# Norm 2's factor spread in two steps, and two unread products behind the attention: a decoder block on one core

## The chip, the cores and the metric

The kernel runs on one core of one Trainium2 chip. A core has a matrix engine (PE in the rows; its weight loads have their own rows, PEld), a vector engine (DVE), a scalar engine (ACT), GpSimd (POOL) and a queue that issues most transfers (SP). The metric is the time of one execution on the device in microseconds (us), the median of several runs.

## What is computed

One layer of a decoder block on 256 tokens of width 2048, in float32. The part around the change, cut from the reference:

```python
h = rms_norm(x, norm1_w[l])
proj = h @ w_in[l]
...                                   # attention (o_nsa) and gated DeltaNet (o_dn) from proj
g_nsa, g_dn = jnp.split(jax.nn.sigmoid(merge_g), 2, axis=-1)
mixed = g_nsa * (o_nsa @ w_up_nsa[l]) + g_dn * (o_dn @ w_up_dn[l])
x = x + mixed @ w_o[l]
h2 = rms_norm(x, norm2_w[l])
x = x + (jax.nn.silu(h2 @ w_ffn_gate[l]) * (h2 @ w_ffn_up[l])) @ w_ffn_down[l]
return rms_norm(x, norm_f_w)
```

`rms_norm` divides each token's row by the root of its mean square. The hidden width of the last three products (the feed-forward part) is 5632.

## The kernel before, in words

**Products.** Weights are read from memory once, in chunks of 1 MB (`load`). Each float32 operand is split into a rounded part `hi` and a remainder `lo` (`split`: ACT writes `hi`, DVE writes `lo`), both of a 4-byte type that TensorE takes in one record per product. A product of two such operands is made of three: hi times hi, lo times hi and hi times lo. An ordinary float32 product, without the split, shows in the trace as two records. A transpose through the identity shows as one.

**Two shapes of the main loop.** `group_t` multiplies with the weights as stationary operand: its line L234 issues products with 256 moving columns. A chunk has two halves; each half issues 24 such products, 16 on `hi` and 8 on `lo`, and then calls `pump`. `group` has the activations as stationary operand and 512 moving columns, on L260, L261 and L262. In the order of the program, the stretches that matter here are:

- the products of the first big matrix on the normalised input (tile `hh`), 256 wide for the most part, with the small products of DeltaNet and attention between them;
- `wud` and `wun` (tiles `odn`, `onsa`): 16 calls of `group_t`, 768 products of 256 columns;
- `wo` (tile `xa`): four calls of `group`, 4 x 4 x 4 x 2 x 3 = 384 products of 512 columns, with transposes of the sum `x1t` on L1196;
- gate and up of the feed-forward part (`wfg`, tile `h`): 88 chunks, 4224 products of 256 columns;
- down (`wd`, tiles `fa` and `fxy`): 4 x 11 x 4 x 2 x 3 = 1056 products of 512 columns.

**What is put between.** Side work runs as Python generators: `pump`, called after each half chunk, takes one step of each lane. So a `yield` moves work by half a chunk. `keep_in_program_order` (`pin`) keeps an instruction at its place on its engine. The attention (`nsa_q`) is such a generator; its last product is `cmp_values` on L923 (tile `oacc`, 96 rows, 512 columns, of the split type).

**Norm 2's factor.** The sum of squares is known when `wo` ends. DVE computes the inverse root in a chain of small operations (`rsqrt`, L275 to L279, tile `r_y`). `row_bcast` then spreads the factors of the two halves of the tokens over the partitions: for each half one float32 product of the broadcast factor with the identity (L1053, tile `R`), and one copy out of PSUM by DVE (L1055). Here the generator that calls it:

```python
def bcast2():
    for _ in range(3):
        yield
    self.R2b = row_bcast(r2, "R2")[:, None, :].to_broadcast([P, 2, 256])
```

It is taken up behind the fourth half chunk of gate and up, where the first gate tile is complete; that tile is multiplied with `R2b` on L1231.

Of the kernel before, what the change touches and what calls it, by code (L numbers as in the profile page):

```python
# [14 lines left out]
P = 128  # L15
# [80 lines left out]
class Kern:  # L96
# [284 lines left out]
    def conv_in(self, e, half, pre):  # L381

        V = self.nc.vector
        if half == 0:
            pre = self.ar.alloc([4, 260], "zm")
            V.memset(pre[:, :, 0:3], 0.0)
        V.tensor_tensor(pre[:, 2 * half:2 * half + 2, 3:259], e, self.R[:, None, :].to_broadcast([P, 2, 256]), op=OP.mult)
        return pre
# [333 lines left out]
    def nsa_kv(self):  # L722
# [16 lines left out]
        kc, vc, ks, kw = self.kvT  # L739
        V.tensor_tensor(vc.ap, vc.ap, self.R[:, None, :].to_broadcast([P, 2, 256]), op=OP.mult)  # L740
        for x in (kc, ks, kw):
# [71 lines left out]
    def nsa_q(self):  # L813
# [141 lines left out]
                yield  # L955
        for v in self.vn:
            v.free()


    def build(self):  # L960
# [82 lines left out]
        def norm_factor(ss, name):  # L1043
            v = self.small([2], name + "v")
            V.tensor_scalar(v[:], ss, 1.0 / D, EPS, op0=OP.mult, op1=OP.add)
            r = self.rsqrt(v[:], [2], name)
            return r

        def row_bcast(r, name):

            bank = self.aux(name)
            for tt in range(2):
                self.pin(nc.tensor.matmul(bank[:, tt * P:(tt + 1) * P], r[:, tt:tt + 1].to_broadcast([P, P]), self.cs["ident"], start=True, stop=True))  # L1053
            R = self.cp.tile([P, 256], F32, name=name)
            V.tensor_copy(R[:], bank[:, :256])  # L1055
            return R

# [4 lines left out]
        rstd1 = self.small([2], "rstd1")  # L1062

        def evac_zab(g, ps):
            w = ZAB_W[g]
            o = 40 if g == 0 else 0
            z0 = sum(ZAB_W[:g]) + o - 40
            for tt in range(2):
                if g == 0:
                    V.tensor_scalar(ab[:, tt, :], ps[tt][:, 0:16], rstd1[:, tt:tt + 1], None, op0=OP.mult)  # L1070
                    V.tensor_scalar(self.gat[:, tt, :], ps[tt][:, 16:40], rstd1[:, tt:tt + 1], None, op0=OP.mult)
                nc.scalar.activation(self.zs[:, tt, z0:z0 + w - o], ps[tt][:, o:w], AF.Silu, scale=rstd1[:, tt:tt + 1])
# [19 lines left out]
        def rms1(ps):  # L1092
            ss = self.small([2], "ssx1")
            V.tensor_reduce(ss[:], ssx[:], axis=AX.X, op=OP.add)
            v = norm_factor(ss[:], "r1")
            V.tensor_copy(rstd1[:], v[:])
            xT.free()
            xn.free()
            evac_zab(0, ps[0])
            yield  # L1100
            evac_zab(1, ps[1])
            yield
            self.R = row_bcast(rstd1, "R1")
            yield from self.dn_small(ab)

        zab = [[t[f"zab{g}"][c] for c in range(4)] for g in range(3)]
        self.add(rows_in())
        ps = self.pair(zab[:2], hact, ZAB_W, first)
        self.add(rms1(ps))
        ps = self.group(zab[2], hact, ZAB_W[2])  # L1110
        evac_zab(2, ps)
# [16 lines left out]
        for n in ("rc", "rs"):  # L1128
            V.tensor_tensor(self.cs[n], self.cs[n], self.R[:], op=OP.mult)

# [55 lines left out]
        for g in range(4):  # L1186
            ps = self.group([t["wo"][g * 4 + c] for c in range(4)], mact)
            cs = slice(g * 512, g * 512 + 512)
            for tt in range(2):
# [3 lines left out]
                bank = self.aux("x1T")  # L1193
# [8 lines left out]
        r2 = norm_factor(sst[:], "r2")  # L1202

        def bcast2():
            for _ in range(3):
                yield
            self.R2b = row_bcast(r2, "R2")[:, None, :].to_broadcast([P, 2, 256])

        self.add(bcast2())
        h2 = lambda k: hh[k // 4][:, :, k % 4, :]  # L1210

# [173 lines left out]
```

## Time and profile before

| | before |
|---|---|
| time, median of 3 runs | 1486.42 us (1485.66 to 1487.04) |
| time of the profiled execution | 1486.53 us |
| its span, first to last instruction | 1484.7 us |
| PE busy, share of the span | 99% |
| DVE, ACT, POOL busy | 61%, 46%, 5% |
| mean granted TensorE clock | 0.998 of full speed |
| DMA, mean rate | 188 GB/s |

The time exceeds the span by 1.8 us, which lies outside the instructions. PE's busy share says little by itself: its records are pipelined, each lasts longer than the distance to the next one, and so a PE that is busy all the time can still issue its products at one distance or another. That distance is read from the start times of rows.

### The profile page before, as it was taken

Reading aid. Unit: us, or ns where it says so; the run is one execution under the profiler, and the core shown is the slowest. Engines: PE = TensorE matmul, PEld = TensorE weight load, DVE = VectorE, ACT = ScalarE, POOL = GpSimd, SP = SyncE. Lnnn points to the kernel's source line nnn. Section 1 sums busy time; section 2 is a strip of 40 time slices with the busy share of each in tenths; the row PEclk is TensorE's granted clock in tenths of the full one; section 3 lists DMA queues with packets and bytes.
Section 4 is the critical chain, followed back from the end, with each engine's and each line's share of the span. In section 5 each row is a group of like instructions: output and inputs, shape, how many; then the busy total and the mean of one; then the engine's idle time right before and its main releaser. Section 6 shows DMA issues by size and latency. Waiting matters only on the chain.

```text
span 1484.7 us, 25996 instructions
## 1 busy us (share of the span) xinstructions
PE 1470.0 (99%) x11017; PEld 1404.8 (95%) x11017; DVE 901.9 (61%) x1352; ACT 688.7 (46%) x850; POOL 78.7 (5%) x69
## 2 busy tenths in 40 slices
PE   9999999999999999999999999999999999999997
PEld 8999999999999999998899999999999998888886
DVE  5679996676787755556655555455555454445444
ACT  5655444445455546444444444444444444444343
POOL 1000101000000000210000000000000000000000
PEclk9999999999999999999999999999999999999999
DMA  8754546345554455455555555555555556555553
GB/s 333 243 195 171 185 171 199 119 166 207 191 194 148 143 199 198 171 199 173 196 178 192 187 182 195 177 196 176 194 185 185 193 179 225 188 188 194 196 198 114
DMA packets 41541, 279.20 MB, mean 188 GB/s; under 512 B 5056, under 2 KB 5584, under 8 KB 9552
## 3 DMA queue, kind: packets, MB, share of 16 engines
q1 hardware_dynamic: 38880, 270.08, 51.9%
q10 hardware_dynamic: 1440, 4.82, 0.9%
q0 software_dynamic: 1104, 2.64, 0.8%
q8 instruction: 86, 1.41, 0.4%
q14 instruction: 31, 0.25, 0.1%
HBM read 274.62 MB, written 2.89 MB: 187 GB/s over the span
## 4 chain that ended last, share of the span: by engine, by line
PE 94%; DVE 3%; DMA 1%; ACT 0%; issue 0%; SPq 0%; DVEq 0%; ACTq 0%
PE mm L234 63%; PE mm L261 8%; PE mm L262 8%; PE mm L260 8%; DVE lo L160 1%; DMA raw<-in_zab 1%; PE oacc L917 1%; PE U L587 1%; DVE main L398 1%; PE pt L903 0%; DVE xs L489 0%; DVE xs L491 0%; PE x1T L1196 0%; PE hid L770 0%; PE hid L771 0%
## 5 line engine op out<-in xcount | busy, mean ns | idle before, releaser
L160 DVE TENSOR_TENSOR lo<-raw,hi 128x1024 fp32r<-128x1024 f32 (+2 forms) x510 | 617.7, 1212 | 440.3 <-ACT hi L159 439.5
L159 ACT ACTIVATE hi<-raw 128x1024 fp32r<-128x1024 f32 (+2 forms) x510 | 533.8, 1048 | 673.1 <-PE mm L234 411.3
L234 PE MATMUL mm<-h,hi 128*128 128x256 f32 x2816 | 360.7, 281 | 0.0
L234 PEld LDWEIGHTS mm<-h,hi 128*128 128x128 f32 x2816 | 344.0, 189 | 0.1
L234 PE MATMUL mm<-hh,hi 128*128 128x256 f32 x2304 | 291.5, 279 | 0.0
L234 PEld LDWEIGHTS mm<-hh,hi 128*128 128x128 f32 x2304 | 275.1, 188 | 0.6 <-ACT hi L159 0.2
L234 PE MATMUL mm<-h,lo 128*128 128x256 f32 x1408 | 194.5, 281 | 0.0
L234 PEld LDWEIGHTS mm<-h,lo 128*128 128x128 f32 x1408 | 178.3, 189 | 0.0
L234 PE MATMUL mm<-hh,lo 128*128 128x256 f32 x1152 | 155.3, 277 | 0.0
L234 PEld LDWEIGHTS mm<-hh,lo 128*128 128x128 f32 x1152 | 142.3, 188 | 0.0
L262 PE MATMUL mm<-hi,fxy 128*128 128x512 f32 x192 | 74.7, 389 | 0.0
L261 PE MATMUL mm<-lo,fxy 128*128 128x512 f32 x192 | 74.7, 389 | 0.0
L260 PE MATMUL mm<-hi,fxy 128*128 128x512 f32 x192 | 74.7, 389 | 0.0
L1233 POOL TENSOR_TENSOR sgt<-sgt,R 128x512 f32<-128x512 f32 x22 | 33.6, 1527 | 548.8 <-ACT sgt L1232 548.8
L260 PE MATMUL mm<-hi,fa 128*128 128x512 f32 x160 | 62.3, 389 | 0.0
L262 PE MATMUL mm<-hi,fa 128*128 128x512 f32 x160 | 62.2, 389 | 0.0
L261 PE MATMUL mm<-lo,fa 128*128 128x512 f32 x160 | 62.2, 389 | 0.0
L261 PE MATMUL mm<-lo,xa 128*128 128x512 f32 x128 | 50.1, 391 | 0.0
L262 PE MATMUL mm<-hi,xa 128*128 128x512 f32 x128 | 50.1, 391 | 0.0
L260 PE MATMUL mm<-hi,xa 128*128 128x512 f32 x128 | 49.8, 389 | 0.0
L261 PE MATMUL mm<-lo,hh 128*128 128x354 f32 (+2 forms) x128 | 44.7, 350 | 0.6 <-DVE lo L160 0.5
L260 PE MATMUL mm<-hi,hh 128*128 128x354 f32 (+2 forms) x128 | 44.1, 351 | 1.2 <-ACT hi L146 1.2
(341 smaller groups left out, 1358.5 us busy)
## 6 DMA issues: line engine op xcount, KB each, us to landing
raw<-in_wfg SPq DMA_DIRECT2D x88, 1024.0 KB, 4.7
raw<-in_wd SPq DMA_DIRECT2D x44, 1024.0 KB, 4.7
raw<-in_wmg SPq DMA_DIRECT2D x32, 1024.0 KB, 4.7
raw<-in_wdn SPq DMA_DIRECT2D x24, 1024.0 KB, 4.8
raw<-in_nsa SPq DMA_DIRECT2D x16, 1024.0 KB, 4.8
raw<-in_wo SPq DMA_DIRECT2D x16, 1024.0 KB, 4.8
raw<-in_wud SPq DMA_DIRECT2D x8, 1024.0 KB, 4.8
raw<-in_wun SPq DMA_DIRECT2D x8, 1024.0 KB, 4.8
```

The costliest lines, as they stand in the source:

```text
L159: nc.scalar.activation(hv, rv[:, m * h:m * h + m, :], AF.Copy)
L160: nc.vector.tensor_tensor(lv, rv[:, m * h:m * h + m, :], hv.bitcast(F32), op=OP.subtract)
L234: nc.tensor.matmul(ps[:, f], (hv, hv, lv)[p][:, k, f * P:f * P + P], a[:, p % 2, :], start=c + h + p + k == 0, stop=c == n - 1 and h + p + ...
L260: nc.tensor.matmul(o, a[:, 0, sl], hv[:, k, :], start=begin, stop=False)
L261: nc.tensor.matmul(o, a[:, 0, sl], lv[:, k, :], start=False, stop=False)
L262: nc.tensor.matmul(o, a[:, 1, sl], hv[:, k, :], start=False, stop=last)
L398: V.scalar_tensor_tensor(cT[:, f, :], pre[:, f, j:j + 256], cw[:, o + j:o + j + 1], cT[:, f, :], op0=OP.mult, op1=OP.add)
L587: nc.tensor.matmul(bv[:, j, :], Pm[t, hg][:, j, :], U[t, hg][:, j, :], start=True, stop=True)
L917: nc.tensor.matmul(ov[:, j, :], self.vn[kb][:, c:c + 128], pt[:, br * nb + kb, :], start=j == 0 and br == 0 and kb == 0, stop=False, skip_ ...
L1233: nc.gpsimd.tensor_tensor(sgt[:], sgt[:], self.R2b, op=OP.mult)
```

## The change

`row_bcast` becomes a generator. With `steps=2`, used for norm 2 alone, it yields between its two products, so that one half chunk of gate and up stands between them; `bcast2` waits two steps in place of three, so the second product stays where the pair stood and the first moves half a chunk forward. A new `kick` issues two float32 products of the identity with itself into a PSUM bank that nothing reads, behind the attention's last product.

```diff
         for v in self.vn:
             v.free()
+        self.kick()
+
+    def kick(self):
+
+        bank = self.aux("kick")
+        for _ in range(2):
+            self.pin(self.nc.tensor.matmul(bank[:, :P], self.cs["ident"], self.cs["ident"], start=True, stop=True))
...
-        def row_bcast(r, name):
+        def row_bcast(r, name, steps=1):
 
             bank = self.aux(name)
             for tt in range(2):
                 self.pin(nc.tensor.matmul(bank[:, tt * P:(tt + 1) * P], r[:, tt:tt + 1].to_broadcast([P, P]), self.cs["ident"], start=True, stop=True))
+                if tt == 0 and steps == 2:
+                    yield
...
-            self.R = row_bcast(rstd1, "R1")
+            self.R = yield from row_bcast(rstd1, "R1")
...
         def bcast2():
-            for _ in range(3):
+            for _ in range(2):
                 yield
-            self.R2b = row_bcast(r2, "R2")[:, None, :].to_broadcast([P, 2, 256])
+            R2 = yield from row_bcast(r2, "R2", 2)
+            self.R2b = R2[:, None, :].to_broadcast([P, 2, 256])
```

On PE, at the end of the attention, these instructions stood before the change (`mm` are the main loop's PSUM tiles; what stands in brackets is whom an instruction waits for):

```order
L234 MATMUL mm_6370<-hh,lo_6470 128x256 [waits DVE_49]
L234 MATMUL mm_6370<-hh,lo_6470 128x256 x7
L923 MATMUL oacc_6232<-zkh 128x512 [waits DVE_49]
L234 MATMUL mm_6503<-odn,hi_6506 128x256 [waits Activation_49]
L234 MATMUL mm_6503<-odn,hi_6506 128x256 x15
```

and these now:

```order
L234 MATMUL mm_6370<-hh,lo_6470 128x256 [waits DVE_49]
L234 MATMUL mm_6370<-hh,lo_6470 128x256 x7
L923 MATMUL oacc_6232<-zkh 128x512 [waits DVE_49]
L964 MATMUL kick_6501<-consts 128x128 x2
L234 MATMUL mm_6506<-odn,hi_6509 128x256 [waits Activation_49]
L234 MATMUL mm_6506<-odn,hi_6509 128x256 x15
```

The two products stand directly behind L923, with no main-loop product between and with no wait of their own.

On PE, at the start of gate and up (third and fourth half chunk, then the first of the next tile), these stood before:

```order
L234 MATMUL mm_8172<-h_7509,lo_8234 128x256 x7
L234 MATMUL mm_8172<-h_7509,hi_8261 128x256 [waits Activation_49]
L234 MATMUL mm_8172<-h_7509,hi_8261 128x256 x7
L234 MATMUL mm_8172<-h_7509,hi_8261 128x256 [waits DVE_49]
L234 MATMUL mm_8172<-h_7509,hi_8261 128x256 x7
L234 MATMUL mm_8172<-h_7509,lo_8262 128x256 x8
L1053 MATMUL R_8289<-consts,r_y_8159 128x128 [waits DVE_49,PE_49]
L1053 MATMUL R_8289<-consts,r_y_8159 128x128
L234 MATMUL mm_8298<-h_7509,hi_8301 128x256 [waits Activation_49]
```

and these now:

```order
L234 MATMUL mm_8175<-h_7512,lo_8237 128x256 x7
L1060 MATMUL R_8264<-consts,r_y_8162 128x128 [waits DVE_49,PE_49]
L234 MATMUL mm_8175<-h_7512,hi_8266 128x256 [waits Activation_49]
L234 MATMUL mm_8175<-h_7512,hi_8266 128x256 x15
L234 MATMUL mm_8175<-h_7512,lo_8267 128x256 x8
L1060 MATMUL R_8264<-consts,r_y_8162 128x128
L234 MATMUL mm_8301<-h_7512,hi_8304 128x256 [waits Activation_49]
```

The first product of the pair, with its wait for DVE's chain, now stands 24 products earlier; the second stands where it stood. On DVE, ACT, POOL and SP every instruction keeps its place.

## Rows read from the trace of the kernel before

**Rows 1.** The profile's page: the span, the busy time of PE and its weight loads, and the granted TensorE clock in 40 slices (9 is 90% or more).

```profile
span 1484.7 us, 25996 instructions
PE 1470.0 (99%) x11017; PEld 1404.8 (95%) x11017; DVE 901.9 (61%) x1352; ACT 688.7 (46%) x850; POOL 78.7 (5%) x69
PEclk9999999999999999999999999999999999999999
```

**Rows 2.** PE's products of L234 in two stretches (`wud` and `wun`; gate and up behind the two products of L1053). Columns: stretch in us, its length, busy time and number of products, granted clock, DMA share, GB/s.

```profile
557.23:647.69 90.46, 90.46 (x768) 1.00 0.53 186
750.10:1236.37 486.27, 486.27 (x4128) 1.00 0.53 187
```

**Rows 3.** PE's instructions in order of time at the start of gate and up. Columns: start, time from the first start to the last end, engine, line, operation, number of records.

```profile
744.30 1.98 PE L234 MATMUL mm<-h,hi 128*128 128x256 f32 x16
...
747.02 1.98 PE L234 MATMUL mm<-h,hi 128*128 128x256 f32 x16
...
749.74 0.60 PE L1053 MATMUL R<-consts,r_y 128*128 128x128 f32 x4
750.10 2.13 PE L234 MATMUL mm<-h,hi 128*128 128x256 f32 x16
...
753.01 2.05 PE L234 MATMUL mm<-h,hi 128*128 128x256 f32 x16
...
755.84 2.05 PE L234 MATMUL mm<-h,hi 128*128 128x256 f32 x16
```

**Rows 4.** The same view around the attention's last product.

```profile
554.27 1.98 PE L234 MATMUL mm<-hh,hi 128*128 128x256 f32 x16
...
556.99 0.40 PE L923 MATMUL oacc<-zkh 96*128 96x512 f32 x1
557.23 2.05 PE L234 MATMUL mm<-odn,hi 128*128 128x256 f32 x16
...
560.06 2.05 PE L234 MATMUL mm<-odn,hi 128*128 128x256 f32 x16
```

**Rows 5.** The same view around an earlier L923, with transposes (L903) just ahead of it.

```profile
529.76 0.60 PE L903 MATMUL pt<-consts,main 128*128 128x128 f32 x4
530.12 0.47 PE L923 MATMUL oacc<-zkh 96*128 96x512 f32 x1
530.43 1.99 PE L234 MATMUL mm<-hh,hi 128*128 128x256 f32 x16
532.26 1.07 PE L234 MATMUL mm<-hh,lo 128*128 128x256 f32 x8
```

**Rows 6.** The same view around two blocks of four float32 products each (L444, DeltaNet), one half chunk apart.

```profile
122.44 1.07 PE L234 MATMUL mm<-hh,lo 128*128 128x256 f32 x8
123.35 1.05 PE L444 MATMUL G<-main 128*128 128x128 f32 x8
...
126.12 1.11 PE L234 MATMUL mm<-hh,lo 128*128 128x256 f32 x8
127.07 1.06 PE L444 MATMUL G<-main 128*128 128x128 f32 x8
...
129.79 1.07 PE L234 MATMUL mm<-hh,lo 128*128 128x256 f32 x8
130.70 0.50 PE L234 MATMUL mm<-hh,hi 128*128 128x256 f32 x3
```

**Rows 7.** The same view around transposes that PE had to wait for (L532; in brackets the idle time ahead and who ended it) and eight float32 products (L546), and the ACT instruction that was waited for.

```profile
190.15 1.06 ACT L402 ACTIVATE main<-main 128x1024 f32<-128x1024 f32 x1 [1.22 <-DVE main L398]
...
191.26 1.09 PE L532 MATMUL qtr<-consts,main 128*128 128x128 f32 x8 [1.39 <-ACT main L402]
...
198.55 1.10 PE L234 MATMUL mm<-hh,lo 128*128 128x256 f32 x8
199.49 1.95 PE L546 MATMUL A<-main 128*128 128x128 f32 x16
...
203.10 1.07 PE L234 MATMUL mm<-hh,lo 128*128 128x256 f32 x8
204.01 1.18 PE L234 MATMUL mm<-hh,hi 128*128 128x256 f32 x9
```

**Rows 8.** The same view around four float32 products of the attention (L917).

```profile
502.49 1.16 PE L917 MATMUL oacc<-main 128*128 128x128 f32 x8
...
505.31 1.07 PE L234 MATMUL mm<-hh,lo 128*128 128x256 f32 x8
506.22 0.29 PE L837 MATMUL sc<-zkh,zq 128*128 128x272 f32 x1
```

**Rows 9.** The end of DVE's chain for norm 2's factor (L279), and the weight loads of the half chunk ahead of which the first product now stands.

```profile
747.04 0.16 DVE L279 SCALAR_TENSOR_TENSOR r_y<-r_u,r_y 128x2 f32<-128x2 f32 x1
...
746.91 1.89 PEld L234 LDWEIGHTS mm<-h,hi 128*128 128x128 f32 x16
```

**Rows 10.** Products of 512 columns: the first and the fourth L260 of a short stretch with `hh` (nine products from the one to the other), and the first and the last L260 of the down stretch (1053 products from the one to the other).

```profile
248.88 0.39 PE L260 MATMUL mm<-hi,hh 128*128 128x512 f32 x1
...
250.94 0.39 PE L260 MATMUL mm<-hi,hh 128*128 128x512 f32 x1
...
1236.37 0.40 PE L260 MATMUL mm<-hi,fa 128*128 128x512 f32 x1
...
1475.07 0.39 PE L260 MATMUL mm<-hi,fa 128*128 128x512 f32 x1
```

## The prediction

> **What bounds the kernel now.** I read the page first. PE is busy for 99% of the span, its weight loads for 95%, and the granted clock stands at full speed (2.4 GHz, the upper of its two levels) in every slice [rows 1]. DVE and ACT are busy for 61% and 46%: they follow PE. So the time is the number of PE's products times the distance from one start to the next, and anything that is neither fewer products nor a smaller distance is worth little.
>
> The second view was the order of time on PE, and there the distance is the thing to see. At the start of gate and up, half chunks of 24 products start at 744.30, 747.02 and (the next break) 749.74: 2.72 us each, 113.3 ns a product [rows 3]. Behind the two products of L1053 the starts are 753.01 and 755.84: 2.83 us, 117.9 ns. It is the same line, the same shape and the same clock. The view by stretches says how long this lasts: 4128 products in 486.27 us are 117.8 ns each, up to the end of gate and up, and the 768 products of `wud` and `wun` in 90.46 us are 117.8 ns each too [rows 2]. Around the attention's last product one sees the same turn: 554.27 to 556.99 is 2.72 us, then L923 stands alone, and 557.23 to 560.06 is 2.83 us [rows 4]. So TensorE runs this loop at one of two distances, which I call the short and the long step. Other products in between can turn one into the other, and then it holds as long as nothing stands in between. The trace does not say why there are two. It shows that the two longest unbroken stretches of L234 both have the long one, and that the change touches exactly the two breaks in front of them.
>
> **What a break does to the step.** The outcomes that can be read:
> - Four float32 products (eight records): short before (122.44 to 123.35, 0.91 us for 8), long behind (126.12 to 127.07, 0.95). Four more, half a chunk later: short again (129.79 to 130.70, 0.91) [rows 6].
> - Two float32 products (L1053): short before, long behind [rows 3].
> - Transposes that PE had to wait for: long behind (198.55 to 199.49, 0.94). Then eight float32 products without a wait: short (203.10 to 204.01, 0.91) [rows 7].
> - L923 alone: short to long [rows 4]. L923 behind transposes: 530.43 to 532.26 is 1.83 us for 16, short apart from the restart [rows 5].
> - A counterexample: four float32 products at 502.49, and behind them the step is short (505.31 to 506.22, 0.91) [rows 8].
>
> From the long step a block of plain float32 products went to the short one each time here (127.07, 199.49). From the short step it mostly went to the long one. That is nearly a switch, and two switches bring the short step back.
>
> **The change part by part.**
>
> *The kick* adds two float32 products, the shape of the pair on L1053, which took 749.74 to 750.10, 0.36 us; the half chunk behind that pair took 2.91 us against 2.83 (750.10 to 753.01), a restart of 0.08 [rows 3]. So it costs 0.44 us on PE with nothing to hide it. It waits for nothing of its own. What it can give: L923 turns short to long, and the float32 block behind it, as at 127.07, turns it back. With the short step 768 products take 768 x 2.72 / 24 = 87.04 us in place of 90.46: -3.42. That no main-loop product stands between L923 and the kick is the weak point. The nearest row, where L923 shares its break with other products, ended short [rows 5].
>
> *The first product of the pair* moves in front of the half chunk whose weight load starts at 746.91. It needs `r_y`, which DVE finishes at 747.04 + 0.16 = 747.20 [rows 9]. From release to start there were 0.05 us in the trace (190.15 + 1.06 = 191.21, PE at 191.26) [rows 7]. So PE will stand for about 747.25 - 746.91 = 0.34 us, and a load that nothing covers adds up to 0.11 (747.02 - 746.91). I take 0.4, with bounds of 0.3 and 0.5. Queued behind it are 24 products of L234 and, through them, the `hi` and `lo` splits for later chunks; they shift by the same 0.4. The copy on DVE waits for the second product, which stays where it was. Splitting the pair costs a second restart, 0.08 (bounds 0 and 0.1).
>
> *The effect of the two steps.* The first, met after a wait, should leave the long step, as the waited transposes did and as the pair did; the second, 24 products later, should turn it to the short step, as at 127.07, also 24 products after a turn. The half chunk between costs 2.83 - 2.72 = 0.11. If instead the first leaves the short step, this 0.11 is saved and the second must leave it too. No row shows a lone float32 product of 128 columns between two half chunks, so this is worked out from blocks of two, four and eight. With the short step the 4128 products take 4128 x 2.72 / 24 = 467.84 us in place of 486.27: -18.43.
>
> *What the short step costs elsewhere.* The loops with 512 columns have two distances as well, and in the opposite sense. Entered from the short step, L260 stands at 248.88 and, nine products later, 250.94: 228.9 ns. Entered from the long step, the down stretch ran from 1236.37 to 1475.07 in 1053 products: 226.7 ns [rows 10]. If the step is handed on like this, down loses 1056 x 2.2 ns = 2.33 us and `wo` 384 x 2.2 = 0.85. The bounds are zero (it falls back, for `wo` at its first transposes) and these. I take them in full, because the code at the entry is the same in both rows.
>
> *The sum*, against the profiled execution's own 1486.53 us: + 0.44 (kick) - 3.42 (`wud`, `wun`) + 0.85 (`wo`) + 0.4 + 0.08 + 0.11 (wait, restart, half chunk) - 18.43 (gate and up) + 2.33 (down) = 1468.89. The median of the runs is 0.11 below the profiled execution, so 1468.8.
>
> [...]
>
> **The rivals.**
> - *Gate and up turn, `wud` and `wun` don't* (L923 and the kick act as one break that ends long): 1486.53 + 0.44 + 0.59 - 18.43 + 2.33 = 1471.5. For it: the break is of a kind that no row shows.
> - *The kick turns, the pair in two steps doesn't*: 1486.53 + 0.44 + 0.59 - 3.42 + 0.85 = 1485.0. For it: the block at 502.49 stayed on one step, and the wait lets the first product start at a moment that no row fixes; a first product that leaves the short step and a second that switches end long.
> - *Neither turns, the change does nothing it could be for*: 1486.53 + 0.44 + 0.59 = 1487.6. [...] Against it: breaks of float32 products changed the step at most places.
> - *Slower*: gate and up keep the long step, but down starts at another moment and takes the 228.9 ns, as does `wo`: 1487.6 + 2.33 + 0.85 = 1490.7. It decides from 3.0 us on, so it needs the down stretch at 2 ns more per product without the 4.5 ns less in front of it. Against it: long was followed by 226.7 [rows 10].
>
> **How the numbers follow.** The forecast (both turn) has 0.55, the first rival 0.20, the second 0.12, the third 0.09, the fourth 0.04. A measurement of this kernel tells 0.2%, 3.0 us, from no change. Forecast and first rival are faster by more: 0.75. The second (-0.10%) and third (+0.07%) are within it: 0.21. The fourth is slower: 0.04. The likeliest case alone runs from 1465.5 (no price on the 512-wide loops) to 1469.5. The two faster cases hold only 0.75, so the range reaches on to the second rival: 1465.0 to 1485.5, which leaves out 0.13.
>
> **What would show it.** In the changed kernel's trace: `wud` and `wun` in about 87 us, gate and up behind the second product in about 468; half chunks of 2.72 us behind `kick` and behind the second product of the pair; an idle time of 0.3 to 0.5 us on PE in front of the first, ended by DVE; L260 of the down stretch 228.9 ns apart. The prediction is wrong if half chunks behind the second product take 2.83 us, which alone is worth 18 us, or if other engines cannot follow the short step and PE begins to wait for `hi` or `lo` in gate and up.

## The result, and the profile after

The changed kernel takes 1470.05 us (1469.73 to 1470.9), against 1486.28 us (1485.66 to 1487.04) for the kernel before in the same comparison: a ratio of 0.9891, with a 95% interval of 0.9874 to 0.9909. It is 1.1% faster. The forecast of 1468.8 lies 1.25 us below the median and the range holds it, but the way to this time is not the one forecast. One execution of a variant below (1607.18 us, at a granted clock of 0.85) and one of the kernel before (5213.38 us) stand far outside, and the ratios leave them out.

The page after; it answers to [rows 1].

```profile
span 1467.9 us, 26004 instructions
PE 1452.7 (99%) x11021; PEld 1386.9 (94%) x11021; DVE 902.1 (61%) x1352; ACT 689.5 (47%) x850; POOL 78.8 (5%) x69
PEclk9999999999999999999999999999999999999999
```

PE has four records more than before, and is busy 17.3 us less; its share and the granted clock have not moved. So neither the busy share nor the clock tells these two kernels apart. The distance between starts does. The same two stretches of L234 as in [rows 2] (stretch, length, busy time and number of records, granted clock, DMA share, GB/s):

```profile
558.13:648.66 90.53, 90.53 (x768) 1.00 0.53 185
751.61:1219.55 467.94, 467.94 (x4129) 1.00 0.56 194
```

`wud` and `wun` have kept the long step: 90.53 us, against 90.46 before. Gate and up behind the second product has the short one: 467.94 us where it had 486.27, that is 18.33 us less. (The 4129th record is the last `lo` product ahead of the stretch: it starts at 751.36, in front of L1060, and by its record ends 0.02 us inside the window.)

PE in order of time around the kick, the changed [rows 4]:

```profile
557.52 0.40 PE L923 MATMUL oacc<-zkh 96*128 96x512 f32 x1
557.76 0.61 PE L964 MATMUL kick<-consts 128*128 128x128 f32 x4
558.13 2.13 PE L234 MATMUL mm<-odn,hi 128*128 128x256 f32 x16
561.04 2.05 PE L234 MATMUL mm<-odn,hi 128*128 128x256 f32 x16
563.86 2.05 PE L234 MATMUL mm<-odn,hi 128*128 128x256 f32 x16
```

The kick takes 0.37 us to the next start, and the half chunk behind it 2.91 (558.13 to 561.04); the next one takes 2.82 (561.04 to 563.86), the long step. And around the pair, with DVE's last step of norm 2's factor, which answer to [rows 3, 9]:

```profile
747.11 1.07 PE L234 MATMUL mm<-h,lo 128*128 128x256 f32 x8
748.35 0.46 PE L1060 MATMUL R<-consts,r_y 128*128 128x128 f32 x2 [0.17 <-DVE r_y L279]
...
750.53 1.10 PE L234 MATMUL mm<-h,lo 128*128 128x256 f32 x8
751.47 0.38 PE L1060 MATMUL R<-consts,r_y 128*128 128x128 f32 x2
751.61 2.07 PE L234 MATMUL mm<-h,hi 128*128 128x256 f32 x16
...
754.43 1.98 PE L234 MATMUL mm<-h,hi 128*128 128x256 f32 x16
```

```profile
748.04 0.16 DVE L279 SCALAR_TENSOR_TENSOR r_y<-r_u,r_y 128x2 f32<-128x2 f32 x1
```

The eight `lo` products at 747.11 would let the next start at 747.11 + 8 x 0.1133 = 748.02. `r_y` ends at 748.04 + 0.16 = 748.20, and PE starts at 748.35: a wait of 0.33 us. (The 0.17 in brackets counts from the modelled end of the last `lo` product, 747.11 + 1.07 = 748.18, and not from the next possible start.) Eight `lo` products take 0.94 between the two parts of the pair (750.53 to 751.47: long step), and the half chunk behind the second takes 2.82 (751.61 to 754.43: 2.72 and a restart). In this execution the first product turned short to long and the second turned it back.

The ledger, by the same starts in both kernels:

| Start of | before | after | later by |
|---|---|---|---|
| L923, last product of the attention | 556.99 | 557.52 | 0.53 |
| the first product with `odn` | 557.23 | 558.13 | 0.90 |
| gate and up, first product | 737.76 | 738.76 | 1.00 |
| the first half chunk behind the pair | 750.10 | 751.61 | 1.51 |
| down (L260) | 1236.37 | 1219.55 | -16.82 |
| end of the span | 1484.7 | 1467.9 | -16.8 |

The program ahead of L923 is the same in both, so the 0.53 is no cost of the change: over the fourteen profiles of this study L923 starts anywhere between 555.99 and 559.83. From there to the pair the change costs 0.98, and in gate and up it gains 18.33.

### The profile page after: what moved, and what is told of

The parts are those of the page before. It is cut to its first block, busy times and chain, and to the rows that moved or that the text cites. A ratio compares the mean times of both kernels' runs of the same rounds, so it can differ in the third digit from the quotient of the medians.

```text
span 1467.9 us, 26004 instructions
## 1 busy us (share of the span) xinstructions
PE 1452.7 (99%) x11021; PEld 1386.9 (94%) x11021; DVE 902.1 (61%) x1352; ACT 689.5 (47%) x850; POOL 78.8 (5%) x69
## 4 chain that ended last, share of the span: by engine, by line
PE 93%; DVE 4%; DMA 2%; issue 1%; ACT 0%; SPq 0%; POOL 0%; DVEq 0%; ACTq 0%; POOLq 0%
PE mm L234 62%; PE mm L261 9%; PE mm L262 9%; PE mm L260 9%; DVE lo L160 2%; DMA raw<-in_zab 1%; PE oacc L917 1%; PE U L587 1%; DVE main L398 0%; DVE xs L489 0%; DVE xs L491 0%; PE pt L903 0%; DMA xs<-scrM 0%; PE x1T L1205 0%; PE hid L770 0%
## 5 line engine op out<-in xcount | busy, mean ns | idle before, releaser
L234 PE MATMUL mm<-h,hi 128*128 128x256 f32 x2816 | 348.6, 276 | 0.0
L234 PEld LDWEIGHTS mm<-h,hi 128*128 128x128 f32 x2816 | 332.6, 188 | 0.1
L234 PE MATMUL mm<-hh,hi 128*128 128x256 f32 x2304 | 292.0, 279 | 0.0
L234 PEld LDWEIGHTS mm<-hh,hi 128*128 128x128 f32 x2304 | 275.5, 188 | 0.6 <-ACT hi L159 0.2
L234 PE MATMUL mm<-h,lo 128*128 128x256 f32 x1408 | 188.2, 276 | 0.0
L234 PEld LDWEIGHTS mm<-h,lo 128*128 128x128 f32 x1408 | 172.7, 188 | 0.0
L234 PE MATMUL mm<-hh,lo 128*128 128x256 f32 x1152 | 155.5, 277 | 0.0
L234 PEld LDWEIGHTS mm<-hh,lo 128*128 128x128 f32 x1152 | 142.4, 188 | 0.0
L260 PE MATMUL mm<-hi,fxy 128*128 128x512 f32 x192 | 74.7, 389 | 0.0
L260 PE MATMUL mm<-hi,fa 128*128 128x512 f32 x160 | 62.2, 389 | 0.0
L260 PE MATMUL mm<-hi,xa 128*128 128x512 f32 x128 | 49.8, 389 | 0.0
L260 PE MATMUL mm<-hi,hh 128*128 128x354 f32 (+2 forms) x128 | 43.8, 348 | 1.5 <-ACT hi L146 1.5
```

The costliest lines, as they stand in the source:

```text
L234: nc.tensor.matmul(ps[:, f], (hv, hv, lv)[p][:, k, f * P:f * P + P], a[:, p % 2, :], start=c + h + p + k == 0, stop=c == n - 1 and h + p + ...
L260: nc.tensor.matmul(o, a[:, 0, sl], hv[:, k, :], start=begin, stop=False)
```

## The experiments

The names used below: *the first* and *the second* are the two products of norm 2's factor, each a float32 product of 128 columns with two records; *the pair* is both together. "Short to long" says which step stood ahead of a break and which behind it. The step is read from the eight `lo` products ahead of a break (0.91 us is short, 0.94 or 0.95 long) and from the first half chunk behind it (2.82 or 2.83 us is the short step and a restart, 2.90 or 2.91 the long step and a restart; a half chunk without a break ahead of it takes 2.72 or 2.83). Each edit is against the changed kernel; `...` stands for hunks that are not shown.

**The split without the kick.** The call in `nsa_q` is gone; the split pair stays.

```diff
         for v in self.vn:
             v.free()
-        self.kick()
```

> The two unread products are taken out; norm 2's pair stays in two steps. In the changed kernel wud and wun still took the long step (90.53 us for 768 products, against 90.46 before), so the theory is that the whole gain comes from the pair in two steps: gate and up behind the second product in 468 us, wud and wun in 90.5 us, 0.45 us less than the changed kernel, so 1469 to 1470.5. Rival: the unread products work from afar (they set the step with which the 512-wide loop and gate and up are entered): then gate and up goes back to 486 us and the time to 1487.

Median 1470.78 us, ratio 0.9918 (0.9883 to 0.9953). Seven of ten executions took 1468.97 to 1472.26 us and three took 1485.83 to 1487.8. PE in order of time in the profiled one, which took 1471.33:

```profile
750.06 0.46 PE L1059 MATMUL R<-consts,r_y 128*128 128x128 f32 x2 [0.17 <-DVE r_y L279]
...
752.19 1.07 PE L234 MATMUL mm<-h,lo 128*128 128x256 f32 x8
753.10 0.38 PE L1059 MATMUL R<-consts,r_y 128*128 128x128 f32 x2
753.23 2.08 PE L234 MATMUL mm<-h,hi 128*128 128x256 f32 x16
...
756.05 1.98 PE L234 MATMUL mm<-h,hi 128*128 128x256 f32 x16
```

So the split alone is worth the whole gain, where it comes out. But the way is another one: eight `lo` products take 0.91 between the two (752.19 to 753.10), which is the short step. Here neither product turned it. And the same program has two times, 17 us apart.

**The kick without the split.** The pair stands together at its old place, the kick stays.

```diff
-            for _ in range(2):
+            for _ in range(3):
                 yield
-            R2 = yield from row_bcast(r2, "R2", 2)
+            R2 = yield from row_bcast(r2, "R2")
```

> The pair stands together again, behind the fourth half chunk; the two unread products stay behind L923. Theory: gate and up takes the long step (486 us), wud and wun too (90.5 us), the time is that of before plus 0.45: 1486.5 to 1487.5. Rival (the unread products work from afar): gate and up in 468 us, about 1469.

Median 1487.68 us, ratio 1.0003 (0.9993 to 1.0013): no difference from before. PE in order of time behind the pair:

```profile
750.36 0.60 PE L1060 MATMUL R<-consts,r_y 128*128 128x128 f32 x4
750.72 2.13 PE L234 MATMUL mm<-h,hi 128*128 128x256 f32 x16
...
753.63 2.05 PE L234 MATMUL mm<-h,hi 128*128 128x256 f32 x16
```

The half chunk behind the pair takes 2.91 us, and the one behind the kick as well (557.73 to 560.64). L923 and the kick together end long, as L923 alone does before the change, and the pair together turns short to long, as before the change.

**A third step.** The split without the kick, and one more unread product on the identity, half a chunk behind the second. If each break were a switch, two would bring the short step and a third would lose it.

```diff
...
             self.R2b = R2[:, None, :].to_broadcast([P, 2, 256])
+            yield
+            self.pin(nc.tensor.matmul(self.aux("k3")[:, :P], self.cs["ident"], self.cs["ident"], start=True, stop=True))
```

> As the pair in two steps without the unread products behind the attention, and one more unread float32 product of the identity half a chunk behind the second. If each such block turns the step, three turns end long: the 24 products between second and third in 2.72 us after the restart, and from there half chunks of 2.83 us; gate and up in about 486 us, the time about 1487.5. If a single product always leaves the short step behind it, or if it is the early place of the first that counts, gate and up stays at 468 us and the time at 1469.5 to 1470.5.

One execution, 1487.9 us. The time is the one that a switch would give, but PE in order of time shows that it isn't one:

```profile
750.12 1.10 PE L234 MATMUL mm<-h,lo 128*128 128x256 f32 x8
751.06 0.38 PE L1059 MATMUL R<-consts,r_y 128*128 128x128 f32 x2
...
753.17 1.10 PE L234 MATMUL mm<-h,lo 128*128 128x256 f32 x8
754.11 0.38 PE L1218 MATMUL k<-consts 128*128 128x128 f32 x2
754.25 2.13 PE L234 MATMUL mm<-h,hi 128*128 128x256 f32 x16
...
757.16 2.05 PE L234 MATMUL mm<-h,hi 128*128 128x256 f32 x16
```

0.94 from `lo` to the second (750.12 to 751.06), 0.94 from `lo` to the third (753.17 to 754.11), 2.91 behind it: long at all three places. The first turned short to long, and then two lone products in a row changed nothing. The run says nothing of what a third product does from the short step.

**The pair early, together.** The split without the kick in its place and its wait, but with both products in one step, half a chunk earlier than before.

```diff
...
-            R2 = yield from row_bcast(r2, "R2", 2)
+            R2 = yield from row_bcast(r2, "R2")
```

> Both products of the pair together, half a chunk earlier than before the change, so with the wait for DVE's chain; no unread products. If the number of turns counts, one block is one turn: short to long, gate and up with half chunks of 2.83 us (489 us over 4152 products), the time 1486.5 to 1487.5. If the early place or the wait is what brings the short step, half chunks of 2.72 us follow and the time is about 1469.5.

One execution, 1486.84 us, PE in order of time:

```profile
747.11 0.68 PE L1059 MATMUL R<-consts,r_y 128*128 128x128 f32 x4 [0.17 <-DVE r_y L279]
747.54 2.13 PE L234 MATMUL mm<-h,hi 128*128 128x256 f32 x16
...
750.45 2.05 PE L234 MATMUL mm<-h,hi 128*128 128x256 f32 x16
```

The same wait of DVE as in the changed kernel, and the long step behind it. In this run neither the earlier place nor the wait makes the gain; what is left is that the two products stand apart. It is one execution, and the split itself misses now and then (below).

**The changed kernel again.** No edit; four executions, one of them profiled.

> The changed kernel as it is, in more executions. With the pair in two steps and without the unread products, 7 executions of 10 took 1469 to 1472 us and 3 took 1486 to 1488. Theory: the first product of the pair meets a wait, so it starts at a moment that differs from one execution to the next, and what step follows is a matter of chance in the changed kernel too: some of its executions at 1486 to 1488 us, some three in ten. Rival: the unread products behind the attention fix the moment, and every execution is at 1469 to 1471 us.

1468.93, 1469.08, 1469.31 and 1470.86 us; ratio 0.9881 (0.9867 to 0.9896). Behind the kick the step is long again. But this profile takes the way of the split alone:

```profile
749.58 0.46 PE L1060 MATMUL R<-consts,r_y 128*128 128x128 f32 x2 [0.17 <-DVE r_y L279]
...
751.71 1.07 PE L234 MATMUL mm<-h,lo 128*128 128x256 f32 x8
752.62 0.38 PE L1060 MATMUL R<-consts,r_y 128*128 128x128 f32 x2
```

0.91 between the two (751.71 to 752.62) is the short step, and it is short behind the second as well (755.58 to 758.29, 2.71). So one and the same kernel reaches the same time with the first product turning short to long and without.

**The old pair, then one more product.** The pair together at its old place, no kick, and half a chunk later one unread product. The pair turns to the long step for certain, so this asks what a lone product does from there.

```diff
...
+            yield
+            self.pin(nc.tensor.matmul(self.aux("k3")[:, :P], self.cs["ident"], self.cs["ident"], start=True, stop=True))
```

> The pair together at its old place, where it meets no wait; one unread float32 product of the identity half a chunk later; no unread products behind the attention. The pair without a wait was followed by the long step in each of three profiles. If a second block turns the step back, 24 products in 2.83 us follow and then half chunks of 2.72 us; as nothing waits, all executions should agree: 0.2 us for the product, 18.3 us saved, about 1468.5 in all. If one product is too little, all executions at about 1487. Either way no two groups of times.

Median 1487.6 us, ratio 1.0 (0.9991 to 1.001), and all ten executions lie between 1486.48 and 1488.74. PE in order of time:

```profile
753.22 1.11 PE L234 MATMUL mm<-h,lo 128*128 128x256 f32 x8
754.16 0.39 PE L1218 MATMUL k<-consts 128*128 128x128 f32 x2
754.31 2.13 PE L234 MATMUL mm<-h,hi 128*128 128x256 f32 x16
...
757.22 2.05 PE L234 MATMUL mm<-h,hi 128*128 128x256 f32 x16
```

Long ahead of the lone product (0.94), long behind it (2.91). Ten executions of ten without the gain: a lone product does not turn the long step back here.

**The old pair, then four more.** The same with four unread products in place of one.

```diff
...
+            yield
+            k4 = self.aux("k4")
+            for _ in range(4):
+                self.pin(nc.tensor.matmul(k4[:, :P], self.cs["ident"], self.cs["ident"], start=True, stop=True))
```

> As the run before, with four unread products in place of one, half a chunk behind the pair. This is the pattern of DeltaNet's two blocks on L444 (four products, half a chunk, four products), which ended with the short step in every profile so far. Expected: all executions agree at about 1469.2 (0.97 us for four products and the restart, 18.3 us saved). If a block of four behind a block of two does not turn, all at about 1487.5.

Median 1469.82 us (1469.34 to 1470.61), ratio 0.9884 (0.9869 to 0.9899). PE in order of time:

```profile
752.44 1.11 PE L234 MATMUL mm<-h,lo 128*128 128x256 f32 x8
753.38 1.06 PE L1220 MATMUL k<-consts 128*128 128x128 f32 x8
754.19 2.08 PE L234 MATMUL mm<-h,hi 128*128 128x256 f32 x16
...
757.01 1.98 PE L234 MATMUL mm<-h,hi 128*128 128x256 f32 x16
```

0.94 ahead of the four, 2.82 behind them (2.72 and a restart): long to short. So what the trace of before showed for blocks of four and eight, [rows 6, 7], does hold at this place; what does not is to expect it of a block of one.

**The kick half a chunk later.** The pair as before; the two unread products no longer stand right behind L923 but between two half chunks of `wud`.

```diff
         for v in self.vn:
             v.free()
-        self.kick()
...
+        def late_kick():
+            self.kick()
+            yield
+
+        self.add(late_kick())
...
```

> The pair as before the change; the two unread products not right behind L923 but half a chunk into wud. L923 alone leaves the long step. If a block of float32 products turns the long step to the short one when it stands between half chunks, the other 744 products of wud and wun take 84.3 us in place of 87.6, and the time is about 1486.4 + 0.45 - 3.3 = 1483.5, less what the 512-wide loop of wo may lose (0 to 0.85). If two products are too few, wud and wun stay at 90.5 us and the time is about 1487.

One execution, 1486.56 us. The two stretches of L234, the first from behind the kick:

```profile
563.26:647.68 84.42, 84.42 (x744) 1.00 0.53 183
750.11:1236.38 486.27, 486.27 (x4128) 1.00 0.53 187
```

744 products in 84.42 us are 113.5 ns each: the kick turned long to short, where right behind L923 it had brought no short step. Two products are enough when there are main-loop products on both sides of them. The time does not show the 3 us, because L923 already starts 2.8 us later in this execution than in the profile of before (559.83 against 556.99), ahead of every edit. The first and the last L260 of the stretch behind it, up to the first transposes:

```profile
647.68 0.39 PE L260 MATMUL mm<-hi,xa 128*128 128x512 f32 x1
...
670.13 0.39 PE L260 MATMUL mm<-hi,xa 128*128 128x512 f32 x1
```

99 products in 22.45 us are 226.8 ns, entered from the short step. The 512-wide loop does not pay for it.

**Both by blocks.** The late kick and the pair with four products behind it, in one kernel.

> What the runs before point to, together, with no wait anywhere: the two unread products half a chunk into wud, norm 2's pair together at its old place, and four unread products half a chunk behind it. Expected from their traces: wud and wun 744 products in 84.3 us behind the block in place of 87.6 (-3.3, +0.45 for the block), gate and up 4104 products in 465 us in place of 483.4 (-18.3, +0.97), nothing at the 512-wide loops: 1486.9 - 3.3 + 0.45 - 18.3 + 0.97 = 1466.7, in all executions alike, 2.5 to 3 us below the changed kernel. If the short step in wud and wun changes what follows the transposes and the pair, gate and up falls back to 486 us and the time is about 1485.

Median 1467.27 us (1466.86 to 1468.34), ratio 0.9878 (0.9834 to 0.9923), in a comparison where the changed kernel took a median of 1469.75. The two stretches of L234, from behind each block:

```profile
560.87:645.29 84.42, 84.42 (x744) 1.00 0.54 184
751.48:1216.70 465.22, 465.22 (x4104) 1.00 0.55 193
```

Both have the short step, 113.5 and 113.4 ns, and none of the four executions fell back. Its median is the lowest of the study, 2.5 us below that of the changed kernel beside it. The interval of its ratio overlaps with that of the changed kernel; what shows the 2.5 us to be no chance is the stretch, 87.61 us from 557.68 to 645.29, its kick included, against 90.53 for the same 768 products behind the kick.

**The split without the wait.** As the split without the kick, but with one Newton step in norm 2's factor in place of three, so part of that factor's computation is left out and `r_y` is ready in time.

```diff
-    def rsqrt(self, v, shape, tag):
+    def rsqrt(self, v, shape, tag, steps=3):
...
-        for _ in range(3):
+        for _ in range(steps):
...
-            r = self.rsqrt(v[:], [2], name)
+            r = self.rsqrt(v[:], [2], name, 1 if name == "r2" else 3)
```

> The pair in two steps without the unread products behind the attention, and with one Newton step in norm 2's factor in place of three: DVE's chain ends over 1 us earlier, so the first product meets no wait (this leaves out a part of the computation). If the wait is what makes the step a matter of chance (7 of 10 executions short with the wait), all executions now agree: all near 1469 or all near 1486.5. If two groups of times remain, the wait is not it.

Median 1468.48 us (1468.39 to 1471.56), ratio 0.9892 (0.984 to 0.9945). PE in order of time:

```profile
747.31 0.38 PE L1059 MATMUL R<-consts,r_y 128*128 128x128 f32 x2
...
749.36 1.07 PE L234 MATMUL mm<-h,lo 128*128 128x256 f32 x8
750.27 0.38 PE L1059 MATMUL R<-consts,r_y 128*128 128x128 f32 x2
```

The wait is gone (`r_y` ends at 746.31 in this trace, 1.00 us ahead of the first) and neither product turns the short step (0.91 from `lo` to the second, and 2.82 for the half chunk behind it, 750.40 to 753.22). Four of four executions have the gain; with the wait it is 30 of 34 (below), so four cannot tell whether the wait is what makes it a matter of chance.

**The changed kernel a third time, and the split alone a second time.** No edits.

> The changed kernel again, beside the next run on the same chip. 8 of 8 executions were short so far; without the unread products 7 of 11 (the kernel with a third step, which has the same two steps, counted in). If the unread products behind the attention make no difference, some executions of 1486 to 1488 us appear here as well; if all are at 1469 to 1471 again while the run beside it shows both, they may do something that the step of wud and wun does not show.

> The pair in two steps without the unread products, in more executions, beside the changed kernel: two groups of times again, around 1470 (about seven in ten) and around 1487.

The changed kernel: eleven of twelve executions from 1468.84 to 1472.44 us, one at 1486.51; ratio 0.9898 (0.9871 to 0.9925). The split alone: four from 1469.43 to 1470.05, ratio 0.9894 (0.985 to 0.9938). The execution at 1486.51 is the one that was profiled, so the trace shows what a miss looks like:

```profile
749.03 1.10 PE L234 MATMUL mm<-h,lo 128*128 128x256 f32 x8
749.98 0.38 PE L1060 MATMUL R<-consts,r_y 128*128 128x128 f32 x2
750.12 2.13 PE L234 MATMUL mm<-h,hi 128*128 128x256 f32 x16
...
753.02 2.05 PE L234 MATMUL mm<-h,hi 128*128 128x256 f32 x16
```

Short to long at the first, long to long at the second (0.95 ahead of it, 2.90 behind), and it stayed so to the end of gate and up. In all, 19 of 20 executions of the changed kernel have the gain and 11 of 14 of the split alone. (The run with a third step, long behind its second product, is not counted.) The kernel before, in turn, took 1469.08 us in one of the 53 executions that it was compared by; no trace shows that one.

## Why the prediction was right, and where it was not

**What is borne out.** There are two distances at one granted clock, other products between two half chunks can turn one into the other, and the one that follows then holds over thousands of products. Gate and up was forecast to give 18.43 us and gave 18.33. The wait was forecast at 0.4 and measured 0.33, with 0.15 us from the end of `r_y` to PE's start where the prediction took 0.05. Wait, second restart and half chunk together were forecast at 0.59 and measured 0.51 (1.51 later behind the pair, less the 1.00 by which gate and up began later). The kick's own cost is 0.37 + 0.08 = 0.45, forecast 0.44.

**The kick: the step that failed.** "L923 turns short to long, and the float32 block behind it, as at 127.07, turns it back": -3.42 became nothing (90.53 against 90.46; the 0.07 is the restart that the kick's 0.45 already holds). All four profiles that have the kick there show the long step behind it. The weak point that the prediction named, no main-loop product between L923 and the kick, was the point: with a half chunk between them the same two products did turn the step, in both profiles that have it so. Which of L923 and the kick leaves the long step where they stand together, no run tells. The case that came is the first rival, which had a chance of 0.20, and not the forecast with its 0.55.

**The 512-wide loops: the step that made up for it.** The prices of 2.33 for down and 0.85 for `wo` were read off a stretch of nine products [rows 10]. Down after the change, first and last L260:

```profile
1219.55 0.39 PE L260 MATMUL mm<-hi,fa 128*128 128x512 f32 x1
...
1458.24 0.39 PE L260 MATMUL mm<-hi,fa 128*128 128x512 f32 x1
```

(1458.24 - 1219.55) / 1053 = 226.7 ns, as before, though entered from the short step. So the price of down is zero. In `wo` it was not due here, since the step ahead of it stayed long; the late kick shows that it is zero there too. Why the short stretch at 248.88 ran at 228.9 ns is open. The seven stretches of twelve such products that follow it in the trace of before, all behind other products than L234, keep 228 ns as well (six from 254.80 to 256.17, for one), so it goes with these stretches with `hh`, and `wo` and down do not have it from either step.

**The sum, put right.** The first rival without the price on down is 1486.53 + 0.44 + 0.59 - 18.43 = 1469.1, and with the 0.53 us by which L923 began later 1469.7; the profiled execution took 1469.73. The forecast came within 1.25 us by luck: two errors, +3.4 on the kick and -3.2 on the 512-wide loops (the latter with `wo`), nearly cancel.

**"That is nearly a switch": a step that is wrong as a picture.** The prediction had the first product turn short to long and the second turn it back, by rows of blocks of four and eight. Of the five profiles in which the split brought the gain (two of the changed kernel, two of the split alone, one without the wait), only the first one of the changed kernel went that way. The table counts these breaks over all the profiles of the study, that of before included; the products in it are float32 ones.

| Break between two half chunks | step ahead | short behind | long behind |
|---|---|---|---|
| the first, alone | short | 4 | 3 |
| the second, alone | short | 4 | 0 |
| the second, a third or the one behind the pair, alone | long | 1 | 4 |
| both together | short | 0 | 7 |
| two unread products (late kick) | long | 2 | 0 |
| four unread products | long | 2 | 0 |

Blocks of two and four between half chunks switched each time at these places (not everywhere: [rows 8]). A lone float32 product left the step as it was in 12 of 16 breaks. (L923, a lone product of another type and shape, turned short to long in all ten profiles in which it stands alone.) So what the change does, above all, is to take away a break that turned short to long in all seven profiles that have it, and to put in its place two breaks which mostly don't. The prediction had this as its other way ("if instead the first leaves the short step ... the second must leave it too", where "leaves" means that the short step follows) and gave it no chance of its own.

**What its chances did not hold** is that the outcome is a matter of the single execution. Its sum and its rivals treated the turn as one thing for every execution; only the second rival came near it, with a wait that "lets the first product start at a moment that no row fixes". The moment turns out to be fixed: in all six profiles that have the split with the wait, the first product starts 1.24 us after the first of the eight `lo` products ahead of it (747.11 to 748.35 in the changed kernel, 748.34 to 749.58 in its second profile), and PE goes on 0.21 or 0.22 us later; three of the six are long behind it and three short. So the length of the wait, as far as the trace resolves it, does not tell the two outcomes apart. For the pair together and for the blocks the turn is nearly fixed: 52 of the 53 executions of the kernel before and 10 of 10 with the lone product behind the pair are long, 8 of 8 with the four products (in two kernels) are short. The split brings the gain in 30 of 34.

**What stays open.** Why there are two distances; why the first product, behind a wait of the same length, comes out differently from one execution to the next, and whether it takes the wait for that; whether the kick changes the odds (1 miss in 20 with it, 3 in 14 without, too few to tell). If it does nothing for them, it is 0.45 us spent for nothing.

## What to carry to other kernels

Where PE is the bound, read the distance between starts in each long stretch and compare it with other stretches of the same line and shape; a busy share of 99% and a full clock hide a difference of 4%. Look at which break stands just ahead of a stretch with the longer distance, and try to split it or to add a small block of other products between two main-loop groups; the blocks that worked here met no wait, and whether a wait would matter is open. Here four unread products at a cost of 0.8 us were worth 17 us, and two at 0.4 were worth 3 (90.46 to 87.61). Time such a kernel over many executions, since a break that mostly comes out well still loses all of its gain when it doesn't.

## What the runs showed of the hardware that was not expected

- One and the same product, 128 x 256 with a weight load of its own, runs at 113.4 or 117.8 ns from start to start with the granted clock at 1.00 in both, and keeps either over more than 4000 products.
- Which of the two follows a lone float32 product behind a wait varies between executions of one program: short in one profile of the changed kernel, long in two. The time varies with where gate and up ends up: 1468.84 and 1486.51 us for the changed kernel on one chip.
- Added work can shorten a kernel: eight records on the identity that nobody reads, half a chunk behind the pair, took 1487.3 us (before) to 1469.8 in the same comparison.
